# A hybrid GLA and neighbourhood-attention block on one core: the residual stream feature major from load to store

## The chip, the core and the metric

The kernel runs on one core of a Trainium2 chip. TensorE (PE) multiplies a stationary 128x128 block with a moving operand of up to 512 columns and sums in PSUM; VectorE (DVE), ScalarE (ACT) and GpSimd (POOL) work on 128 lanes; SyncE (SP) issues the transfers between DRAM and SBUF. The metric is the device time of one execution in microseconds, the median over runs.

## What is computed

Two layers over 512 latent tokens (a grid of 8 rows of 64) and 256 context tokens, width 1024, all in fp32. Layer 0 mixes tokens by gated linear attention in both directions (4 heads), layer 1 by neighbourhood attention (16 heads, latent tokens attend to a window and to the context). Each is followed by a gated feed-forward with a depthwise convolution of width 3 (2816 hidden features). Cut to what matters:

```
def modulate(x, g, shift, scale):             # rms_norm divides by the root of the mean square over features
    return rms_norm(x, g) * (1 + scale) + shift

for i in range(2):
    sh1, s1, g1, sh2, s2, g2 = split(silu(c) @ ada_w[i] + ada_b[i], 6)   # the same with c_ctx for the context
    h = modulate(x, norm1_g[i], sh1, s1)
    o = gla_mixer(h_ctx, h_lat) if i == 0 else na_mixer(h_ctx, h_lat)
    x = x + g1 * o                             # context only in layer 0
    h = modulate(x, norm2_g[i], sh2, s2)
    x = x + g2 * conv_ffn(h)                   # context only in layer 0
return rms_norm(x_lat, final_g)
# gla_mixer ends in (rms_norm(o, norm_g) * silu(r)) @ w_out, na_mixer and conv_ffn in a product with their w_out
```

## The kernel before

**Precision.** Each large product is made of three matmuls (`mm3`, L249 to L252): both operands are split into a high part and a low part (`split_to` L261: a ScalarE copy makes the high part, a VectorE subtraction the low part), and low x high, high x low and high x high are summed in PSUM. `wunit` (L234) loads a tile of weights of 128x1024, 512 KB, and splits it in the same way (L245, L246).

**Layouts.** The residual stream `X` is token major: six tiles of 128 tokens x 1024 features, two of context and four latent. What the products read, `H`, is feature major: eight tiles of 128 features x 768 tokens, high and low. So each norm turns its result: `normed` (L278) squares a token tile on ScalarE with a running sum along the row, makes the reciprocal root on GpSimd (L290, L293) and scales the row (L297); `norm_pair` (L302) turns two token tiles with TensorE (L316), applies scale and shift of the modulation, which lie along lanes then (`affine` L270), and splits.

**Gates and output products.** Token major, a gate of the residual add varies along the row. `gate_rows` (L221) therefore makes it a full 128x512 tile by TensorE (L227). Layer 0 multiplies the product with it and adds (`add_gated` L333: L338, L339); in layer 1 GpSimd multiplies the output weights with it as they are loaded (L242), and only the add remains (L335). The output products hold a token tile of activations stationary and move 512 columns of weights past it. In linear attention GpSimd also multiplies each head's result with the norm's weight `gnB` (`silu_r` L602, at L611) ahead of the product with the gate of silu (L612).

**Order of the stages.** Start: six tiles of `x` are loaded, normed, turned (L352), while `ada_first` (L129) makes the first modulation from four tiles of weights (L140, L143, L148); then the first projections. Linear attention runs head by head, `part_a` and `part_b`, levels of blocks whose decays VectorE makes (L536 to L543) for small TensorE products (L514); the last head's stretches are filled with turns and with the first half of the output product (`turn_early`). `finish_gla` reloads `x`, ends the output product and makes the second norm. `ffn` goes over 22 blocks of 128 hidden features in seven groups, six of three and one of four: two input products for each, convolution on VectorE, then the group's output product is added to `X`; in the last group the following norm (`after`) is interleaved tile by tile. Modulations for later come from `ada_lanes` (L182), in which VectorE sums weight rows (L195) in the course of other stages. Attention runs over head pairs with output products in between; its last ones are interleaved with the next norm. `final` norms a token tile and stores it.

**What sets the order.** The code is written in an order, and a list scheduler then chooses each engine's row of instructions from it; each engine works through its row strictly. Buffers are pools: three PSUM banks `mm`, five `aux`, three staging buffers for weights, five split weight tiles, four temporaries `t2`.

The split that all large products use:

```
def mm3(out, a, b, first, last):
    mm(out, a[1], b[0], start=first, stop=False)
    mm(out, a[0], b[1], start=False, stop=False)
    mm(out, a[0], b[0], start=False, stop=last)
```

## Time and profile before

| | before |
|---|---|
| median of 3 runs | 1756.88 us (1753.84 to 1758.1) |
| the profiled execution | 1755.54 us, its span 1753.8 us |
| mean granted TensorE clock | 0.993 |
| PE busy | 1695.0 us, 97% of the span |
| DVE busy | 1107.6 us, 63% |
| ACT busy | 663.1 us, 38% |
| POOL busy | 331.8 us, 19% |
| moved by DMA | 177.73 MB, mean 101 GB/s |

Busy time is a share of the whole span, and the stages have different limits, so the rows further down go by stretches. A matmul record lasts from its start to its modelled end and overlaps the next; what one costs is the spacing of starts. Where a row ends in square brackets, the engine stood idle so long before it, and the name behind the arrow is what it waited for.

### The profile page before, as it was taken

The page shows a single profiled execution, that of the slowest core. Times are in us where ns is not written, and L with a number is a line of the kernel's source. Part 1 is how long each engine was busy: PE and PEld are TensorE (multiplying, and loading weights), DVE is VectorE, ACT ScalarE, POOL GpSimd, SP SyncE. Part 2 cuts the span into 40 slices and gives each one's busy share as a digit, 9 for nine tenths or more (in the row PEclk, how much of TensorE's full clock was granted, in tenths as well). Part 3 has the DMA queues.
Part 4 walks back from the last instruction along what each step waited for, and adds up shares of the span by engine and source line. Part 5 has one row for each costly group of instructions (what it writes and reads, how often), then busy time and mean ns, then how long its engine had stood idle before and what let it go on. Part 6 is the DMA issues. An engine that isn't in the chain of part 4 may idle for free.

```text
span 1753.8 us, 26851 instructions
## 1 busy us (share of the span) xinstructions
PE 1695.0 (97%) x10783; PEld 1442.9 (82%) x10783; DVE 1107.6 (63%) x1666; ACT 663.1 (38%) x1227; POOL 331.8 (19%) x476
## 2 busy tenths in 40 slices
PE   6999999989999999999999999999999899999998
PEld 4767778777799998989899978888888788888887
DVE  4697877876656867685665484445455665566555
ACT  4675655652531221212122254443434432223322
POOL 2042423231100000000000024333442211222221
PEclk9999999999999999999999999999999999999999
DMA  8553423016122534554242212112110132233231
GB/s 292 154 169 121 148 84 113 19 49 216 49 73 92 173 112 128 181 156 142 75 132 61 73 41 88 58 41 65 54 61 25 61 115 87 87 109 108 96 96 49
DMA packets 52749, 177.73 MB, mean 101 GB/s; under 512 B 6864, under 2 KB 8784, under 8 KB 52624
## 3 DMA queue, kind: packets, MB, share of 16 engines
q1 hardware_dynamic: 52624, 176.01, 31.4%
q8 instruction: 85, 1.39, 0.3%
q14 instruction: 40, 0.33, 0.1%
HBM read 171.79 MB, written 2.10 MB: 99 GB/s over the span
## 4 chain that ended last, share of the span: by engine, by line
PE 79%; DVE 9%; ACT 4%; issue 3%; DMA 2%; POOL 2%; SPq 0%; DVEq 0%; POOLq 0%; ACTq 0%
PE mm L250 18%; PE mm L252 17%; PE mm L251 17%; PE aux L250 6%; PE aux L251 6%; PE aux L252 6%; PE mm L1013 2%; DMA sa<-in 2%; PE aux L996 2%; PE aux L971 2%; DVE t L543 1%; PE aux L623 1%; DVE t L537 1%; PE aux L316 1%; PE aux L587 1%
## 5 line engine op out<-in xcount | busy, mean ns | idle before, releaser
L250 PE MATMUL mm<-hh,wl 128*128 128x384 f32 (+3 forms) x976 | 344.7, 354 | 5.2 <-ACT hh L262 4.1
L251 PE MATMUL mm<-hl,wh 128*128 128x384 f32 (+3 forms) x976 | 340.0, 348 | 0.2
L252 PE MATMUL mm<-hh,wh 128*128 128x384 f32 (+3 forms) x976 | 339.8, 348 | 0.0
L245 ACT ACTIVATE wh<-st 128x1024 fp32r<-128x1024 f32 (+1 forms) x197 | 204.2, 1052 | 311.4 <-PE mm L252 171.2
L246 DVE TENSOR_TENSOR wl<-st,wh 128x1024 fp32r<-128x1024 f32 (+1 forms) x196 | 243.5, 1247 | 36.8 <-ACT wh L245 36.2
L250 PEld LDWEIGHTS mm<-hh,wl 128*128 128x128 f32 (+1 forms) x976 | 183.5, 188 | 27.8 <-issue 5.1
L250 PE MATMUL aux<-hh,wl 128*128 128x384 f32 (+2 forms) x576 | 200.3, 348 | 0.0
L252 PE MATMUL aux<-hh,wh 128*128 128x384 f32 (+2 forms) x576 | 200.0, 347 | 0.0
L251 PE MATMUL aux<-hl,wh 128*128 128x384 f32 (+2 forms) x576 | 199.9, 347 | 0.0
L251 PEld LDWEIGHTS mm<-hl,wh 128*128 128x128 f32 (+1 forms) x976 | 184.0, 189 | 16.8 <-DVE hl L263 1.9
L252 PEld LDWEIGHTS mm<-hh,wh 128*128 128x128 f32 (+1 forms) x976 | 183.9, 188 | 15.1
L250 PE MATMUL mm<-wh,ul 128*128 128x512 f32 (+1 forms) x444 | 176.2, 397 | 4.7 <-DVE ul L263 4.7
L251 PE MATMUL mm<-wl,uh 128*128 128x512 f32 (+1 forms) x444 | 174.9, 394 | 0.0
L252 PE MATMUL mm<-wh,uh 128*128 128x512 f32 (+1 forms) x444 | 174.3, 395 | 0.0
L242 POOL TENSOR_TENSOR st<-st,gB 128x512 f32<-128x512 f32 x60 | 94.9, 1610 | 267.3 <-DMA st<-in 139.9
L290 POOL TENSOR_SCALAR ms<-ss 128x1 f32<-128x1 f32 x26 | 9.0, 346 | 631.5 <-ACT xn L288 630.9
L250 PE MATMUL mm<-wh,hl 128*128 128x512 f32 x288 | 116.6, 405 | 0.8 <-ACT wh L245 0.8
L250 PEld LDWEIGHTS aux<-hh,wl 128*128 128x128 f32 x576 | 108.3, 188 | 9.0 <-issue 1.8
L802 ACT ACTIVATE apad<-mm 128x256 f32<-128x256 f32 (+3 forms) x90 | 36.5, 433 | 208.9 <-PE mm L252 208.9
L251 PE MATMUL mm<-wl,hh 128*128 128x512 f32 x288 | 114.8, 399 | 0.0
L251 PEld LDWEIGHTS aux<-hl,wh 128*128 128x128 f32 x576 | 108.4, 188 | 7.4 <-issue 0.4
L252 PE MATMUL mm<-wh,hh 128*128 128x512 f32 x288 | 114.3, 397 | 0.0
(211 smaller groups left out, 2826.9 us busy)
## 6 DMA issues: line engine op xcount, KB each, us to landing
st<-in SPq DMA_DIRECT2D x196, 512.0 KB, 3.7
sa<-in SPq DMA_DIRECT2D x98, 512.0 KB, 4.2
sx<-in SPq DMA_DIRECT2D x14, 512.0 KB, 6.4
xl<-in SPq DMA_DIRECT2D x8, 512.0 KB, 7.1
xc<-in SPq DMA_DIRECT2D x4, 512.0 KB, 4.4
out<-xn SPq DMA_DIRECT2D x8, 256.0 KB, 2.0
raw<-in SPq DMA_DIRECT2D x16, 96.0 KB, 2.4
t<-q SPq DMA_DIRECT2D x16, 64.0 KB, 2.1
```

The source lines that it names most:

```text
L242: nc.gpsimd.tensor_mul(st[:, s_], st[:, s_], gate[half])
L245: nc.scalar.activation(hi, st, AF.Copy)
L246: (eng or nc.vector).tensor_sub(lo, st, hi.bitcast(F32))
L250: mm(out, a[1], b[0], start=first, stop=False)
L251: mm(out, a[0], b[1], start=False, stop=False)
L252: mm(out, a[0], b[0], start=False, stop=last)
L316: nc.tensor.transpose(ps[:, o:o + 128], xs[m][k // 4][:, (k % 4) * 128:(k % 4) * 128 + 128], ident)
L537: nc.vector.tensor_sub(v(eq)[:, :, 0, :], v(bB)[:, :, 0, :], cB)
L802: nc.scalar.activation(apad[j % 2][:, pad_of(p0):pad_of(p1 - 1) + 1], ps[:, p0 - a:p1 - a], AF.Copy)
L971: mm(pss[hh][:, off:off + 256], qe[a_][p_, 128 * t:128 * t + 128], ke[b_][p_, ks], start=i == 0, stop=i == 2)
L996: nc.tensor.transpose(pT[:, i * 128:(i + 1) * 128], S2[:, o:o + 128], ident)
L1013: mm(po[64 * hh:64 * hh + 64, 128 * t:128 * t + 128], V[:, vs[i], 64 * hh:64 * hh + 64], PTs[hh][:, i * 128:(i + 1) * 128], start=i == 0, ...
```

## The change

`X` becomes feature major. `x` and `ctx` arrive turned (two context tiles that hold four feature tiles of 256 tokens each, four latent tiles that hold two feature tiles of 512 tokens each), and the output leaves as 1024 features x 512 tokens.

- A gate is then a number for each lane: `add_gated` is one VectorE instruction. `gate_rows` and the products of weights and gate are gone.
- A norm (`Norm`) sums squares over feature tiles (`add`), sums over lanes with a TensorE product with ones, makes the roots, spreads them over the lanes with a second product (`stats`), and scales, shifts and splits each feature tile (`apply`). No result of a norm is turned.
- Output products hold the weights stationary and move tokens: 8 feature tiles times a latent range of 512 and a context range of 256 tokens; in the last group of the second feed-forward and in the last one of attention two halves of 256. The first feed-forward's input products take the ranges 512 + 256 in place of 384 + 384.
- The norm weight of linear attention goes into the output weights (`scales` in `wunit`), and the product with `gnB` is gone. Five of the eight output weight tiles are loaded twice, once for each range.
- The output is stored in 16 transfers of 128 KB in place of 8 of 256 KB.

```diff
-    def wunit(src, gate=None, eng=None):
+    def wunit(src, eng=None, scales=None):
...
-        if gate:
-            for half in range(2):
-                s_ = slice(half * 512, half * 512 + 512)
-                nc.gpsimd.tensor_mul(st[:, s_], st[:, s_], gate[half])
...
+        if scales:
+            for i in range(2):
+                s_, h_, l_ = (t_.rearrange("p (k i n) -> p k i n", i=2, n=128)[:, :, i, :] for t_ in (st, hi, lo))
+                nc.scalar.activation(h_, s_, AF.Copy, scale=scales[i])
+                nc.vector.scalar_tensor_tensor(l_, s_, scales[i], h_.bitcast(F32), OP.mult, OP.subtract)
+            return hi, lo
...
-    def add_gated(pool, ps, g, xs):
-        if g is None:
-            nc.vector.tensor_add(xs, xs, ps)
-            return
-        tmp = pool.tile([128, 512], F32, name="tmp", tag="t2")
-        nc.vector.tensor_mul(tmp, ps, g)
-        nc.vector.tensor_add(xs, xs, tmp)
+    def gate(l, n, d, rng):
+        return modT[l][:, (3 * n + 2) * 8 + d, 1 if rng[1] <= N_CTX else 0:][:, 0:1]
+
+    def add_gated(ps, l, n, d, rng):
+
+        x_ = xk(d, rng)
+        nc.vector.scalar_tensor_tensor(x_, ps, gate(l, n, d, rng), x_, OP.mult, OP.add)
+
+    class Norm:
...
+        def add(self, k):
+
+            if self.acc is None:
+                self.acc = self.pool.tile([128, self.w], F32, name="nacc", tag=f"nacc{self.w}", bufs=2)
+                nc.scalar.activation(self.acc, xk(k, self.rng), AF.Square)
+                return
+            sq = self.tmp("sq")
+            nc.scalar.activation(sq, xk(k, self.rng), AF.Square)
+            nc.vector.tensor_add(self.acc, self.acc, sq)
+
+        def stats(self):
+
+            c = self.w // 128
+            ps = ps_aux()
+            for i in range(c):
+                mm(ps[:, 2 * i:2 * i + 2], self.acc[:, i * 128:(i + 1) * 128], ones, start=True, stop=True)
+            ms = sml.tile([128, 4], F32, name="ms4", tag="ms4", bufs=2)
+            nc.vector.tensor_scalar(ms[:, 0:c], ps[:, 0:2 * c:2], 1.0 / D, EPS, OP.mult, OP.add)
+            rs = sml.tile([128, 4], F32, name="rs4", tag="rs4", bufs=2)
+            nc.gpsimd.tensor_tensor(rs[:, 0:c], ms[:, 0:c], mhalf.to_broadcast([128, c]), OP.pow)
+            pb = ps_aux()
+            for i in range(c):
+                mm(pb[:, i * 128:(i + 1) * 128], rs[:, i:i + 1].to_broadcast([128, 128]), ident, start=True, stop=True)
...
+        def apply(self, k):
...
+            if self.blocks:
+                nc.vector.tensor_mul(t.rearrange("p (b r c) -> p r b c", r=8, b=8),
+                                     xk(k, self.rng).rearrange("p (r b c) -> p r b c", r=8, b=8),
+                                     self.rb.rearrange("p (r b c) -> p r b c", r=8, b=8))
+                nc.scalar.activation(t, t, AF.Identity, bias=b_, scale=a_)
+                split_to(hi, lo, t)
+                return
+            nc.vector.scalar_tensor_tensor(t, xk(k, self.rng), a_, self.rb, OP.mult, OP.mult)
+            nc.scalar.activation(hi, t, AF.Identity, bias=b_)
+            nc.vector.scalar_tensor_tensor(lo, t, b_, hi.bitcast(F32), OP.add, OP.subtract)
...
-            nc.gpsimd.tensor_mul(yh, yh, gnB)
             nc.gpsimd.tensor_mul(yh, yh, e)
...
+        lat, cx = Norm(pool, 0, 1, LAT), Norm(pool, 0, 1, CTX)
+        units = {}
+        for d in range(KD):
+            w, ps = early[d] if d < 3 else (out_unit(d), ps_mm())
+            out_part(ps, w, LAT, 6 if d < 3 else 0, KD)
+            add_gated(ps, 0, 0, d, LAT)
+            lat.add(d)
+            if d > 4:
+                units[d] = w
+        todo = lat.steps()
+        for d in (5, 6, 7, 0, 1, 2, 3, 4):
+            w = units.get(d) or out_unit(d)
             ps = ps_mm()
+            out_part(ps, w, CTX, 0, KD)
+            todo.pop(0)()
+            add_gated(ps[:, 0:N_CTX], 0, 0, d, CTX)
+            cx.add(d)
+        return todo + cx.steps()
...
-        rngs = ((0, 384), (384, 768)) if l == 0 else ((256, 768),)
+        rngs = (LAT, CTX) if l == 0 else (LAT,)
...
+                todo = []
+                for rng in (LAT, CTX) if l == 0 else ((256, 512), (512, 768)):
+                    norm = after(pool, rng)
+                    for d in range(KD):
+                        ps = out_group(d, rng)
+                        if todo:
+                            todo.pop(0)()
+                        add_gated(ps, l, 1, d, rng)
+                        norm.add(d)
+                    todo += norm.steps()
+                for f in todo:
+                    f()
...
+    class Final(Norm):
+        def apply(self, k):
+            a, b = self.rng
+            y = self.tmp("y")
+            nc.vector.scalar_tensor_tensor(y, xk(k, self.rng), sT[:, R_FG + k:R_FG + k + 1], self.rb, OP.mult, OP.mult)
+            nc.sync.dma_start(outs[0][k, :, a - N_CTX:b - N_CTX], y)
```

VectorE's row at the start, before: each token tile is scaled (`xn`) and copied back from the transposes (`xnT`), then the modulation comes (L121) and the first split.

```order
L297 TENSOR_SCALAR xn<-xl_92,rs 128x512 x2
L358 COPY xnT<-aux 128x4x128
L297 TENSOR_SCALAR xn<-xl_94,rs 128x512 x2
L246 TENSOR_TENSOR wl<-st,wh 128x512
L358 COPY xnT<-aux 128x4x128
L121 TENSOR_TENSOR mod_120<-aux,sT 128x4 x2
L126 SCALAR_TENSOR_TENSOR modA_122<-mod_120,sT 128x4
L276 TENSOR_SCALAR hf<-xnT,modA_122,mod_120 128x512 x2
L246 TENSOR_TENSOR wl<-st,wh 128x1024
L263 TENSOR_TENSOR hl<-hf,hh 128x768 x2
```

The same place after: sums of squares (`nacc`) and two means (L303) in place of scaled and copied tiles.

```order
L294 TENSOR_TENSOR nacc<-nacc,sq 128x512 x7
L303 TENSOR_SCALAR ms_159<-aux 128x4
L294 TENSOR_TENSOR nacc<-nacc,sq 128x256 x7
L303 TENSOR_SCALAR ms_196<-aux 128x2
L245 TENSOR_TENSOR wl<-st,wh 128x512
L129 TENSOR_TENSOR mod_122<-aux,sT 128x4 x2
L134 SCALAR_TENSOR_TENSOR modA_124<-mod_122,sT 128x4
L328 SCALAR_TENSOR_TENSOR hf<-xl_86,modA_124,rb 128x512
L328 SCALAR_TENSOR_TENSOR hf<-xc_84,modA_124,rb 128x256
L245 TENSOR_TENSOR wl<-st,wh 128x1024
L330 SCALAR_TENSOR_TENSOR hl<-hf,mod_122,hh 128x512
```

The modulation's sums no longer stand behind copies from transposes.

VectorE's row from the last context products of the first feed-forward (`xc`) to attention's weights (`wl`), before:

```order
L339 TENSOR_TENSOR xc_4311<-xc_4311,tmp 128x512
L263 TENSOR_TENSOR hl<-hf,hh 128x2x8x32
L338 TENSOR_TENSOR tmp<-mm,gB 128x512
L297 TENSOR_SCALAR xn<-xc_4309,rs 128x512
L339 TENSOR_TENSOR xc_4311<-xc_4311,tmp 128x512
L297 TENSOR_SCALAR xn<-xc_4309,rs 128x512
L246 TENSOR_TENSOR wl<-st,wh 128x1024 x2
L297 TENSOR_SCALAR xn<-xc_4311,rs 128x512 x2
L246 TENSOR_TENSOR wl<-st,wh 128x1024
```

After, with the latent norm's products (L322) and splits (L262) of the last feature tiles:

```order
L245 TENSOR_TENSOR wl<-st,wh 128x1024
L262 TENSOR_TENSOR hl<-hf,hh 128x512
L294 TENSOR_TENSOR nacc<-nacc,sq 128x256
L262 TENSOR_TENSOR hl<-hf,hh 128x512
L322 TENSOR_TENSOR hf<-xl_4231,aux 128x8x8x8
L294 TENSOR_TENSOR nacc<-nacc,sq 128x256
L322 TENSOR_TENSOR hf<-xl_4231,aux 128x8x8x8
L303 TENSOR_SCALAR ms_9397<-aux 128x2
L245 TENSOR_TENSOR wl<-st,wh 128x1024
L262 TENSOR_TENSOR hl<-hf,hh 128x512
L328 SCALAR_TENSOR_TENSOR hf<-xc_4226,modA_125,aux 128x256 x2
L262 TENSOR_TENSOR hl<-hf,hh 128x512
```

Latent splits and products of the norm now stand behind and between the first weights of attention.

VectorE's last rows, before:

```order
L335 TENSOR_TENSOR xl_4317<-xl_4317,mm 128x512 x2
L299 SCALAR_TENSOR_TENSOR xn<-xl_4317,rs,fgB 128x512 x2
L335 TENSOR_TENSOR xl_4319<-xl_4319,mm 128x512
L335 TENSOR_TENSOR xl_4319<-xl_4319,mm 128x256 x2
L299 SCALAR_TENSOR_TENSOR xn<-xl_4319,rs,fgB 128x512 x2
```

And after:

```order
L273 SCALAR_TENSOR_TENSOR xl_4231<-mm,mod_123,xl_4231 128x256
L1109 SCALAR_TENSOR_TENSOR y<-xl_4231,sT,aux 128x256
L294 TENSOR_TENSOR nacc<-nacc,sq 128x256
L303 TENSOR_SCALAR ms_15933<-aux 128x2
L1109 SCALAR_TENSOR_TENSOR y<-xl_4228,sT,aux 128x256 x2
L1109 SCALAR_TENSOR_TENSOR y<-xl_4229,sT,aux 128x256 x2
L1109 SCALAR_TENSOR_TENSOR y<-xl_4230,sT,aux 128x256 x2
L1109 SCALAR_TENSOR_TENSOR y<-xl_4231,sT,aux 128x256 x2
```

Eight outputs of 256 columns stand behind the last mean, where two of 512 stood behind the last root.

## Rows read from the trace of the kernel before

**Rows 1.** Stretches: window, length, busy time of PE, PEld, DVE, ACT, POOL, clock, DMA
```profile
25.00:66.70 41.70, 39.12 (x273) 29.68 (x274) 17.99 (x38) 18.34 (x29) 3.10 (x5) 0.96 0.60 190
66.70:365.00 298.30, 275.77 (x2784) 218.18 (x2784) 247.95 (x371) 184.63 (x379) 93.44 (x94) 0.99 0.34 109
...
1005.00:1060.00 55.00, 54.47 (x268) 43.99 (x267) 41.53 (x70) 27.65 (x59) 14.30 (x32) 1.00 0.22 70
...
1365.00:1400.00 35.00, 30.81 (x208) 26.91 (x207) 20.23 (x34) 17.63 (x39) 9.47 (x20) 1.00 0.24 76
```

**Rows 2.** Timeline of PE: start, length, instruction, shape; pairs that span equal matmuls
```profile
702.06 0.33 PE L250 MATMUL mm<-hh,wl 128*128 128x384 f32 x1
...
704.66 0.33 PE L250 MATMUL mm<-hh,wl 128*128 128x384 f32 x1
...
1371.97 0.98 PE L316 MATMUL aux<-ident,xn 128*128 128x128 f32 x7 [1.07 <-DVE xn L297]
1372.71 0.48 PE L250 MATMUL mm<-wh,ol 128*128 128x512 f32 x1
...
1392.54 0.28 PE L250 MATMUL aux<-hh,wl 128*128 128x256 f32 x1
...
1395.41 0.28 PE L250 MATMUL aux<-hh,wl 128*128 128x256 f32 x1
...
1419.95 0.39 PE L250 MATMUL mm<-wh,ul 128*128 128x512 f32 x1
...
1421.77 0.39 PE L252 MATMUL mm<-wh,uh 128*128 128x512 f32 x1
```

**Rows 3.** Start: timeline of PE, and DMA rate of the first 20 us
```profile
23.32 1.07 PE L140 MATMUL mm<-sx,cs 128*32 128x256 f32 x16
...
28.60 0.56 PE L250 MATMUL mm<-hh,wl 128*64 128x384 f32 x2 [2.38 <-ACT hh L262]
...
GB/s 0 0 0 90 90 185 372 295 393 221 213 262 385 328 377 401 393 418 434 418 410 418 410 418 434 410 410 410 426 426 410 401 401 410 401 410 418 410 426 401
```

**Rows 4.** Linear attention: PE's waits (sum, times, longest), a group, timelines of DVE, POOL
```profile
PE aux L514 <- DVE t L543: 10.4, 10, 3.1
...
L611 POOL TENSOR_TENSOR xl<-xl,gnB 128x256 f32<-128x256 f32 x16 | 27.2, 1701 | 50.1 <-DVE er L609 41.1 <-DVE mod L118 5.8 <-ACT t L541 3.1
...
339.59 1.40 POOL L611 TENSOR_TENSOR xc<-xc,gnB 128x256 f32<-128x256 f32 x1 [1.76 <-DVE er L609]
...
340.31 1.09 DVE L536 TENSOR_TENSOR t<-b 128x384 f32<-128x384 f32 x1
...
342.25 0.55 DVE L537 TENSOR_TENSOR t<-b 128x384 f32<-128x384 f32 x1
```

**Rows 5.** First feed-forward: timeline of PE at and behind a stall
```profile
677.21 0.50 PE L250 MATMUL mm<-wh,ul 128*128 128x512 f32 x1 [2.10 <-DVE ul L263]
...
678.34 0.63 PE L251 MATMUL mm<-wl,uh 128*128 128x512 f32 x1
...
681.33 0.49 PE L250 MATMUL mm<-wh,ul 128*128 128x512 f32 x1
```

**Rows 6.** VectorE's groups by line and shape: sum, mean ns, idle before them
```profile
L246 DVE TENSOR_TENSOR wl<-st,wh 128x1024 fp32r<-128x1024 f32 x195 | 242.8, 1250 | 36.8 <-ACT wh L245 36.2
...
L338 DVE TENSOR_TENSOR tmp<-mm,gB 128x512 f32<-128x512 f32 x96 | 66.1, 690 | 38.9 <-PE mm L252 38.7
...
L843 DVE TENSOR_TENSOR u<-tt,aux 128x256 f32<-128x256 f32 x30 | 12.1, 419 | 17.0 <-ACT tt L838 17.0
...
L629 DVE SCALAR_TENSOR_TENSOR xl<-aux,rs,xl 128x256 f32<-128x256 f32 x16 | 7.5, 480 | 13.1 <-POOL rs L258 13.0
```

**Rows 7.** The end: timeline of PE, POOL and DVE
```profile
1746.81 0.28 PE L252 MATMUL mm<-wh,uh 128*128 128x256 f32 x1
...
1748.66 0.55 POOL L293 TENSOR_TENSOR rs<-ms,mhalf 128x1 f32<-128x1 f32 x1
...
1749.24 1.41 DVE L299 SCALAR_TENSOR_TENSOR xn<-xl,rs,fgB 128x512 f32<-128x512 f32 x2 [1.70 <-POOL rs L293]
```

## The prediction before the run

> **What bounds the kernel now.** I read the table of stretches first [rows 1]: TensorE is busy 275.77 of 298.30 us in the linear-attention stretch, 54.47 of 55 us at the border from the first feed-forward to neighbourhood attention, 30.81 of 35 us at the border behind that attention, and it fills the rest but for the start and the last microseconds. VectorE is busy 247.95 of 298.30 us in linear attention and about three quarters of the time at the first of these borders. So TensorE's own work sets the time, and an edit elsewhere counts only where TensorE waits: at the start, inside linear attention, at the borders where a norm must be finished, and behind the last matmul. The prediction is a sum over these places, made against the profiled run's 1755.54 us, which stands 1.3 us below the median of 1756.88.
>
> **TensorE's work: -9.0.** Records overlap, so I take the spacing of starts [rows 2]: eight 512-wide matmuls in 1.82 us are 0.2275 us each, fifteen 384-wide in 2.60 are 0.173, twenty-four 256-wide in 2.87 are 0.120, and seven 128-wide fp32 records in 0.74 are 0.106. The orders of both kernels, counted, give 1944 more split matmuls of 256 columns, 1920 fewer of 384 and 468 more of 512: +232.5 - 332.7 + 106.5 = +6.3. (384 + 384 becomes 512 + 256 in the first feed-forward, and the output groups that had 512 columns of weights moving now have 512 or 256 tokens moving.) Gone are 128 transposes (L316) outside the start, -13.6, and 48 gate broadcasts (L227) of two records each, -10.2. New are, for each of 20 blocks of 128 tokens outside the start, a sum over lanes (L301) and a broadcast (L308), two records each: +8.5. Spacings read from two rows may be off by 0.005 us, and 468 and 1944 of them make 2 us: I keep -9, from -11 to -7.
>
> The Trainium skill (TensorE: Matmul & The Clock Gate, Back-to-back issue gap) gives N/2.4 + 2.5 ns for an isolated warm matmul, an estimate of 109, 162 and 216 ns for these widths; the rows show about 11 more for each. By it the column term would be +1 and the sum 5 us lower. Its sustained 131 ns for 512 columns is not what these rows show.
>
> **The start: -5, from -6 to -2.** The modulation matmuls that the first products need (L140) end at 24.4, because TensorE takes them between the transposes; then copy, small matmuls, scale, affine and split lead to the first product at 28.60, 4.2 us later [rows 3]. The transfers run at about 400 GB/s from the fifth microsecond [rows 3] (its columns are 0.5 us each); summed, the 5.5 MB of constants, x and the first four modulation tiles have landed at about 17. The changed start has no transposes, and its norm sums hide: eight squares of 512 and eight of 256 on ScalarE follow the x tiles and end near 13.5, statistics near 16. So the modulation matmuls could end near 18.5, the same chain follows, and the first product comes near 23. TensorE then has nearly nothing to wait for until 66.7 (39.12 of 41.70, 2.4 of the rest before the first product), so the gain is kept. -2 if the sums queue ahead of the modulation copies.
>
> **Linear attention: -4, from -8 to 0.** TensorE waits 10.4 us for the decay products (L543) of VectorE there [rows 4]. GpSimd's multiplication by the norm weight (L611, 16 of 1.70 us on the latent half, 8 like them on the context) goes into the output weights. While it runs, a subtraction of two SBUF operands takes 1.09 instead of 0.55 us: the one at 340.31 begins inside the product at 339.59, the one at 342.25 does not overlap it [rows 4]. One such stretch of 0.54 for each of 24 is 13 us of VectorE's time. VectorE is the later engine only in the levels where TensorE waits, so about a third passes on. 0 if the scheduler's order, not VectorE's pace, makes these waits; -8 with the clock's part below.
>
> **A stall costs more than its length.** After the 2.10 us wait in the first feed-forward the 512-wide matmuls are spaced 0.427 us from 678.34 to 681.33, the lower of the clock's two levels (1.2 against 2.4 GHz) [rows 5]: seven by 0.2 more than in [rows 2] are 1.4 us on top. I count this for stalls over 2 us.
>
> **End of linear attention: 0, from -1 to +2.** A context group is 24 matmuls, 2.88 us. VectorE's work for one is a scaled weight tile (the 1.25 of L246, here in two halves with a scalar), two ops of 512 columns for the latent half, one gated 256 (0.48) and one add (0.42): 3.3 [rows 6]. Five of the eight groups load weights anew; the deficit of 5 by 0.4 is covered by the three that do not.
>
> **First feed-forward: +1, from -3 to +5.** The 2.10 us stall there is a wait for a split (L263) [rows 5], in whose row on VectorE the sums of the next modulation (L195, over weights that come from DRAM) stand. These jobs stay. The gate drops from two VectorE ops of 0.69 to one for each block [rows 6], but VectorE doesn't bound these groups, so that is worth nothing; the work ahead of the third split shrinks by about 0.7, so such a stall may grow by that, come twice more with its slow clock, or vanish with it (3.5).
>
> **First feed-forward to neighbourhood attention: +4.5, from +1 to +7.** Before, TensorE is full there [rows 1]. Now the context range comes last: a group is four products in three parts of 256 columns, 1.44 us, and beside each VectorE has a gated 256, an add of 256, a latent product and a latent split of 512: 0.40 + 0.34 + 0.61 + 0.61 = 1.96, from 0.48, 0.42 and twice 0.69 [rows 6] less about 0.08 of overlap each. Eight by 0.52 leave VectorE 4.2 us late, and the weights of attention (1.25 each) and the last latent splits stand behind that in its row. Three accumulators in PSUM let TensorE run ahead, but it then waits at the first projection. Lower end: the scheduler's filling; upper: plus 1.4 of slow clock.
>
> **Attention to the second feed-forward: -1, from -2 to +2.** 35 - 30.81 = 4.2 us of waits are there now [rows 1], behind scale, transpose, affine and split. The last output group in two token halves gives 0.72 us of TensorE against 1.5 of VectorE for each of 16; one half's norm hides beside the other, the second doesn't, about 3.
>
> **The end: +3.5, from +3 to +4.** Now the last matmul starts at 1746.81, the reciprocal root at 1748.66, and the two scaled outputs run from 1749.24 to 1750.65 [rows 7]; 3.1 remain to the span's end. After: gated 0.48, square, add 0.42, lane sum, mean, root 0.55, broadcast, then eight outputs of 256 columns at 0.40 (the four y buffers make the second four wait for transfers), and the same 3.1: about 10.2 from the last matmul's end against 6.7.
>
> **Sum.** -9 - 5 - 4 + 0 + 1 + 4.5 - 1 + 3.5 = -10: a profiled run of 1745.5, a median of 1746. The unknown ends, taken as independent, give 1739 to 1754.
>
> **Rivals.** *VectorE becomes the bound at every norm border (slower).* Price: the whole excess of the last range at each: 5 by 0.7 at the end of linear attention, 4.2 plus 3 of queued weights ahead of attention, 16 by 0.78 behind it, and 1.4 of slow clock at three places, 27 in place of the 3.5 counted: 1769 at worst, 1764 if a quarter hides. It decides if VectorE's share per group exceeds TensorE's by more than the three accumulators cover. For it: 1.96 against 1.44. Against it: the scheduler may put next-stage products between. *The gains at the waits don't land (same).* Linear attention gives 0, the start -2, the border costs 7: -9 - 2 + 0 + 0 + 1 + 7 - 1 + 3.5 = -0.5, 1756. For it: TensorE's waits there follow a hand-made interleave. *GpSimd's product holds VectorE for its whole length.* Then 24 by 1.6 = 39 us of VectorE come free, and all 10.4 us of waits behind L543 go, with the slow clock after the longest: -13 in place of -4, 1737. For it: ops in its shadow double. Against it: 0.54 lost, not 1.4 [rows 4].
>
> The Trainium skill (SBUF — State Buffer, Who interferes with whom) has this third rival as a rule: VectorE reads a second SBUF operand through a port shared with GpSimd, and whichever op comes second is blocked fully. Here the stretch is shorter than the GpSimd op's 1.40 us, so the rows bear out sharing, not a hold over the whole length.
>
> **Chances.** Forecast 0.55, VectorE-bound borders 0.15, no gain at the waits 0.17, full release 0.13. A measurement of this kernel can tell about 0.3%, 5.3 us, from no change. Faster: 0.8 of the forecast, all of the full release, a fifth of "no gain", 0.60. Same: the rest of the forecast, 0.7 of "no gain", a quarter of the slow rival, 0.27. Slower: 0.13. The range 1735 to 1761 takes in the forecast, "no gain", most of the full release and the near side of the slow rival, and leaves out about 0.15.
>
> **What would show it.** In the profile after: first product at 22 to 24; waits behind the decay products near 6 in linear attention; no stall over 1 us at the end of linear attention; one stall of 3 to 6 us where attention's first projections begin, with VectorE's splits or weights as releaser; 3 us in sum behind attention; 10 us from the last matmul to the end. The forecast is wrong if the first product stays near 28, if the borders lose over 12 us together, or if TensorE's sum does not fall by about 9.

## The result, and the profile after

The changed kernel takes 1740.78 us in the median of 6 runs (1738.64 to 1748.47); the kernel before took 1757.24 beside it (1753.3 to 1758.27). The ratio of the mean times, here as for every run below, is 0.9918, with a 95% interval of 0.9896 to 0.994. Between the medians 16.5 us were gained, between the means 14.4, where 11 were forecast. The profiled run took 1739.42 us with a span of 1737.6, 16.2 below the span before.

The table of stretches, cut at the same places in both kernels: start, first product, first decay product, last V·t product of linear attention, first and last modulation sum of the first feed-forward, first scores and end of neighbourhood attention, last matmul, end. The columns are those of [rows 1]: window, length, busy time of PE, PEld, DVE, ACT, POOL, granted clock, DMA share, GB/s. Before:

```profile
0.00:28.60 28.60, 13.85 (x91) 10.29 (x91) 14.14 (x34) 16.66 (x39) 7.27 (x26) 1.00 0.89 321
28.60:90.40 61.80, 60.40 (x403) 45.44 (x403) 36.13 (x63) 33.08 (x59) 3.10 (x5) 0.97 0.52 168
90.40:394.50 304.10, 281.43 (x2783) 224.51 (x2783) 245.38 (x371) 180.02 (x374) 100.64 (x107) 0.98 0.32 101
394.50:560.60 166.10, 163.04 (x862) 141.55 (x861) 101.43 (x148) 56.35 (x104) 9.86 (x29) 1.00 0.30 102
560.60:910.30 349.70, 345.00 (x1856) 318.98 (x1855) 238.66 (x301) 79.22 (x118) 0.00 (x0) 0.99 0.45 142
910.30:1067.60 157.30, 156.77 (x831) 140.49 (x831) 93.18 (x138) 53.39 (x98) 16.98 (x36) 1.00 0.20 63
...
1358.60:1747.10 388.50, 383.79 (x1802) 319.13 (x1800) 230.17 (x275) 125.68 (x185) 80.88 (x70) 1.00 0.28 90
1747.10:1753.80 6.70, 0.00 (x0) 0.00 (x0) 1.83 (x3) 0.71 (x4) 1.16 (x4) 0.71 0.21 79
```

And after:

```profile
0.00:29.45 29.45, 11.95 (x67) 8.31 (x67) 13.10 (x32) 13.30 (x26) 2.71 (x11) 0.97 0.82 306
29.45:92.40 62.95, 61.21 (x400) 45.31 (x400) 44.42 (x78) 32.74 (x60) 3.33 (x5) 0.96 0.51 166
92.40:383.00 290.60, 277.41 (x2784) 221.10 (x2784) 234.63 (x378) 181.12 (x379) 72.38 (x83) 1.00 0.34 106
383.00:543.00 160.00, 156.00 (x907) 137.62 (x906) 101.38 (x152) 55.43 (x89) 5.85 (x14) 0.99 0.39 122
543.00:887.80 344.80, 343.10 (x2000) 297.99 (x1999) 212.69 (x255) 78.69 (x104) 0.00 (x0) 1.00 0.46 144
887.80:1045.30 157.50, 154.69 (x875) 135.16 (x875) 86.12 (x130) 53.69 (x84) 7.92 (x16) 0.99 0.20 62
...
1335.80:1726.60 390.80, 385.62 (x1908) 324.87 (x1908) 224.68 (x330) 125.31 (x183) 3.21 (x7) 1.00 0.28 86
1726.60:1737.60 11.00, 1.32 (x8) 1.04 (x8) 5.03 (x13) 0.42 (x1) 0.69 (x1) 0.70 0.34 119
```

Row by row the lengths differ by +0.85, +1.15, -13.5, -6.1, -4.9, +0.2, +2.3 and +4.3; neighbourhood attention itself, left out here, by -0.5. Linear attention gave most of the gain, at the same count of matmuls: TensorE's idle time (length less busy) fell from 22.7 to 13.2, and its busy time by 4.0 with the granted clock, 0.98 to 1.00. VectorE's busy time fell by 10.8. The start gave nothing. The waits of TensorE (sum, times, longest), the third of which answers to [rows 4]:

```profile
PE aux L301 <- DVE nacc L294: 10.3, 3, 8.5
PE aux L308 <- POOL rs L305: 8.6, 10, 1.5
PE aux L497 <- DVE t L526: 5.8, 7, 1.1
```

The third row was 10.4 before, under L514 and L543. The first two are new (8.5 of the first is at the start, where TensorE waits for the first sums): the sums over lanes and the broadcasts of a norm wait for VectorE's squares and for GpSimd's roots.

### The profile page after: what moved, and what is told of

Same layout as the page of the kernel before. It is cut to its first block, busy times and chain, and to the rows that moved or that the text cites. A ratio compares the mean times of both kernels' runs of the same rounds, so it can differ in the third digit from the quotient of the medians.

```text
span 1737.6 us, 27175 instructions
## 1 busy us (share of the span) xinstructions
PE 1681.7 (97%) x11107; PEld 1413.8 (81%) x11107; DVE 1070.4 (62%) x1699; ACT 658.7 (38%) x1173; POOL 190.9 (11%) x324
## 4 chain that ended last, share of the span: by engine, by line
PE 80%; DVE 10%; ACT 4%; DMA 2%; issue 2%; POOL 1%; SPq 0%; POOLq 0%; DVEq 0%; ACTq 0%
PE mm L249 18%; PE mm L251 17%; PE mm L250 17%; PE aux L249 6%; PE aux L250 6%; PE aux L251 6%; PE mm L1006 2%; DMA sa<-in 2%; PE aux L989 2%; PE aux L964 2%; DVE t L526 1%; PE aux L605 1%; PE aux L570 1%; DVE acc L203 1%; DVE t L525 1%
## 5 line engine op out<-in xcount | busy, mean ns | idle before, releaser
L249 PE MATMUL mm<-hh,wl 128*128 128x512 f32 (+3 forms) x1104 | 388.6, 354 | 3.9 <-ACT hh L329 2.5
L251 PE MATMUL mm<-hh,wh 128*128 128x512 f32 (+3 forms) x1104 | 383.3, 348 | 0.0
L250 PE MATMUL mm<-hl,wh 128*128 128x512 f32 (+3 forms) x1104 | 383.0, 347 | 0.0
L249 PE MATMUL aux<-hh,wl 128*128 128x512 f32 (+2 forms) x576 | 201.1, 349 | 0.0
L250 PE MATMUL aux<-hl,wh 128*128 128x512 f32 (+2 forms) x576 | 201.0, 349 | 0.0
L251 PE MATMUL aux<-hh,wh 128*128 128x512 f32 (+2 forms) x576 | 200.8, 349 | 0.0
L249 PE MATMUL mm<-uh,wl 128*128 128x512 f32 (+1 forms) x560 | 194.1, 350 | 1.7 <-ACT uh L261 1.4
L250 PE MATMUL mm<-ul,wh 128*128 128x512 f32 (+1 forms) x560 | 194.2, 348 | 0.0
L251 PE MATMUL mm<-uh,wh 128*128 128x512 f32 (+1 forms) x560 | 193.3, 346 | 0.0
L273 DVE SCALAR_TENSOR_TENSOR xl<-mm,mod,xl 128x512 f32<-128x512 f32 (+1 forms) x168 | 116.3, 698 | 108.9 <-PE mm L251 108.6
L250 PEld LDWEIGHTS aux<-hl,wh 128*128 128x128 f32 x576 | 109.2, 190 | 14.4 <-issue 1.1
```

What stands on the lines that cost most here:

```text
L273: nc.vector.scalar_tensor_tensor(x_, ps, gate(l, n, d, rng), x_, OP.mult, OP.add)
```

## Experiments

**Linear attention: what did the missing product give?** Two kernels put a GpSimd product of the same size back into the changed kernel, against a tile of ones. In `g_chain` it stands where the old one stood, in the chain of the output; in `g_side` its result goes to a scratch tile that nobody reads. `b_nogn` is the kernel before without L611.

`g_chain`:

```diff
+            nc.gpsimd.tensor_mul(yh, yh, oneB)
             nc.gpsimd.tensor_mul(yh, yh, e)
```

> The changed kernel with one GpSimd product of 128x256 put back for each head and token tile (24 in all), by a tile of ones, in the place where the product with the norm's weight stood. Linear attention is 13.4 us shorter after the change than before. Theory A, VectorE's two-operand instructions are slowed while the product runs and VectorE sets the pace at nearly every wait there: 8 to 13 us slower than the changed kernel, back near 1750. Theory B, the step of the prediction, where only a third of it passes on: 3 to 5 us slower. Theory C, the scheduler's other order made the gain, not the product: within 2 us of the changed kernel.

`g_side`:

```diff
             nc.gpsimd.tensor_mul(yh, yh, e)
+            sc = pool.tile([128, DV], F32, name="sc", tag="sc", bufs=1)
+            nc.gpsimd.tensor_mul(sc, yh, oneB)
```

> The changed kernel with the same 24 GpSimd products of two SBUF operands, written to a scratch tile behind the product with the gate, so that nobody waits for them. Theory A, contention with VectorE is what counts: the same 8 to 13 us as with the product in the chain, VectorE's subtractions of 384 columns at a mean over 0.62 us. Rival D, the product costs because the head's result comes later: within 2 us of the changed kernel, though the other run lost 8 or more.

`b_nogn`, against the kernel before:

```diff
-            nc.gpsimd.tensor_mul(yh, yh, gnB)
             nc.gpsimd.tensor_mul(yh, yh, e)
```

> The kernel before without GpSimd's product with the norm's weight, which leaves that weight out of the result. Theory A: 8 to 13 us faster than the kernel before, with waits behind the decay products near 6 us in place of 10.4. Theory B: 3 to 5 us faster. Theory C: within 2 us of the kernel before.

The table of stretches for linear attention, one row of each, in this order:

```profile
93.40:397.00 303.60, 283.09 (x2784) 226.35 (x2784) 246.60 (x378) 181.51 (x379) 98.81 (x107) 0.98 0.33 102
```
```profile
92.10:392.70 300.60, 279.85 (x2784) 223.77 (x2784) 246.39 (x378) 181.59 (x379) 96.53 (x107) 0.99 0.33 103
```
```profile
90.60:385.00 294.40, 278.80 (x2783) 222.01 (x2783) 233.95 (x371) 180.31 (x374) 69.26 (x83) 0.99 0.33 105
```

Put back in the chain, the product costs 13.0 us of this stretch; put back beside the chain, 10.0; taken out of the kernel before, it gives 9.7. In the kernels below that leave this place alone the stretch takes 290.6 to 294.3, so a difference of 3 to 4 us here shows nothing. The whole times follow: `g_chain` 1750.28 against 1754.72 (0.9965, 0.9949 to 0.9982), `g_side` 1747.60 (0.9956, 0.9939 to 0.9972), `b_nogn` 1745.51 (0.9938, 0.9915 to 0.9962); `g_side` is 6.8 above the changed kernel's median, a little under the 8 that theory A asked for. Most of the gain of linear attention is the missing product, 9.7 to 13.0 us of 13.5, and it works by what it does to VectorE, since the scratch product, for which nobody waits, costs nearly as much. Nor does it make the chain's own products late: of GpSimd's 47.5 us of idle time before those of the latent half, 47.4 are waits for ScalarE. The longer chain explains 3 us at most, which is within the spread. One row of TensorE's waits in `g_side`, of the decay products behind VectorE:

```profile
PE aux L499 <- DVE t L528: 6.1, 7, 1.1
```

That is hardly more than the 5.8 of the changed kernel, though the stretch is 10 us longer: VectorE's loss came out at other waits and in the granted clock (0.99 for 1.00).

**The start: why no gain?** TensorE's timeline of the changed kernel (start, length, instruction, shape, idle before):

```profile
13.08 1.84 PE L301 MATMUL aux<-ones,nacc 128*128 128x2 f32 x8 [8.52 <-DVE nacc L294]
16.37 2.07 PE L308 MATMUL aux<-ident,rs 128*128 128x128 f32 x8 [1.45 <-POOL rs L305]
18.68 1.02 PE L301 MATMUL aux<-ones,nacc 128*128 128x2 f32 x4 [0.23 <-DVE nacc L294]
19.62 1.06 PE L148 MATMUL mm<-sx,cs 128*32 128x256 f32 x2
21.12 1.22 PE L308 MATMUL aux<-ident,rs 128*128 128x128 f32 x4 [0.43 <-POOL rs L305]
22.27 2.96 PE L148 MATMUL mm<-sx,cs 128*32 128x256 f32 x30
...
29.45 0.90 PE L249 MATMUL mm<-hh,wl 128*64 128x384 f32 x2 [2.46 <-ACT hh L329]
```

The modulation's matmuls (L148) end at 25.23, and the first product follows 4.2 us later, as before. Both norms' statistics stand ahead of 30 of the 32 modulation matmuls in TensorE's row. Their four groups last 6.15 us in sum, the first broadcast 2.07 for eight records where [rows 2] show 0.106 for one, and each broadcast waits for roots that GpSimd makes in 1.1 us. ScalarE's last squares come late too, for want of buffers, which come free as VectorE adds; VectorE itself stood 2.02 us at the latent range's mean, for TensorE's sums over lanes. A row of ScalarE, and one of GpSimd:

```profile
15.48 1.48 ACT L293 ACTIVATE sq<-xc 128x256 f32<-128x256 f32 x3 [2.10 <-DVE nacc L294]
```
```profile
15.20 1.12 POOL L305 TENSOR_TENSOR rs<-ms,mhalf 128x4 f32<-128x4 f32 x1 [14.11 <-DVE ms L303]
```

`s_both` writes the modulation's matmuls ahead of the statistics and gives the squares four buffers of their own. `n_ln` shortens the statistics in place: one product of a 128x128 tile of ones with the sums spreads the mean to all lanes at once, and ScalarE makes the root as exp(-0.5 ln). `n_ln_y` adds buffers to it: four and seven for the squares, twelve for the output.

`s_both`:

```diff
+        first = ada_first(0, pool)
         norms = [Norm(pool, 0, 0, rng, spread=True) for rng in (LAT, CTX)]
...
                 norm.add(k)
+        for norm in norms:
             norm.stats()
...
-        ada_first(0, pool)()
+        first()
```

> The changed kernel with the first modulation's matmuls written ahead of the first norm's statistics, both statistics behind both sums, and four staging buffers of their own for the squares of each range. The changed kernel's first product is at 29.45 us, not near 23 as predicted. Theory E, the statistics of the context range stand ahead of the modulation matmuls in TensorE's row, and its sums wait for buffers and for a mean on VectorE: first product at 24 to 26, 3 to 5 us faster than the changed kernel, the gain kept to the end. Rival F, transfers or ScalarE's squares set the start: first product over 28.5, within 1 us.

`n_ln`, in `stats`, with `ones` 128x128:

```diff
-            c = self.w // 128
-            ps = ps_aux()
...
+            ps = ps_aux()[:, 0:self.w]
+            mm(ps, ones, self.acc, start=True, stop=True)
+            self.rb = self.acc
+            nc.scalar.activation(self.rb, ps, AF.Ln, bias=epsc, scale=1.0 / D)
+            nc.scalar.activation(self.rb, self.rb, AF.Exp, scale=-0.5)
```

> The changed kernel with another way through the statistics: one product of a 128x128 tile of ones with the summed squares gives the sum over lanes on every lane at once, and ScalarE makes the reciprocal root by Ln and Exp, in place of lane sum, mean on VectorE, power on GpSimd and broadcast product. s_both left the first product at 30.4 us; the modulation matmuls still stood behind statistics in TensorE's row. Theory E, the statistics in TensorE's row set the start: first product at 23.5 to 25.5, 4 to 6 us of the sum; the end shorter by 1.3, the waits at roots (8.6 us in 10 places) mostly gone, TensorE's statistics cheaper by about 4; in all 8 to 13 us faster than the changed kernel, 1728 to 1733. Rival F, transfers, squares and sums set the start: first product over 28, in all 3 to 7 us faster.

`n_ln_y`, besides:

```diff
+                sq = self.pool.tile([128, self.w], F32, name="sq", tag=f"sq{self.w}", bufs=4 if self.w == 512 else 7)
...
-            y = self.tmp("y")
+            y = self.pool.tile([128, self.w], F32, name="y", tag="y", bufs=12)
```

> n_ln with twelve buffers of their own for the outputs and with four and seven of their own for the first norm's squares. The last eight outputs wait 0.65 us for earlier transfers, and ScalarE waits about 2 us for square buffers at the start. Theory: the end 0.6 us shorter, the first product up to 1.5 us earlier than in n_ln if the context range's sum is last there, 0 if the modulation's transfers are. Rival: transfers follow each other at their own rate at the end, no change.

`s_both` took 1738.90 (0.9899, 0.9875 to 0.9924), but its first product came at 30.4: the expectation missed. The scheduler still wove the statistics into the modulation in TensorE's row: 24 of its 32 matmuls stand behind the second sum over lanes, 16 behind the last broadcast. It doesn't settle the start; its 3 us lie elsewhere and are within what stretches without an edit vary by. `n_ln` moved the first product to 24.94:

```profile
12.76 2.04 PE L301 MATMUL aux<-nacc,ones 128*128 128x512 f32 x2 [7.80 <-DVE nacc L296]
...
17.33 3.30 PE L150 MATMUL mm<-sx,cs 128*32 128x256 f32 x32
24.94 0.90 PE L251 MATMUL mm<-hh,wl 128*64 128x384 f32 x2 [2.53 <-ACT hh L321]
```

The modulation ends at 20.63, 4.6 earlier than in the changed kernel, and the first product follows 4.3 behind it. So the statistics in TensorE's row were what held the start. `n_ln` took 1734.12 (0.988, 0.9865 to 0.9894), `n_ln_y` 1732.22 (0.9876, 0.9859 to 0.9892); the added buffers did not bring the first product further forward (26.5). The price of Ln and Exp shows at the norms of layer 1. ScalarE's timeline at the end of `n_ln_y`:

```profile
1718.84 1.28 ACT L306 ACT_TABLE_LOAD   x1
```

A second load of 1.28 us stands at 1721.22, before the Exp. The last matmul stood 12.4 us from the end, and 13.3 in `n_ln`, where the changed kernel has 11.0 and 1.3 less were expected; the way from the feed-forward to attention took 160.5 instead of 157.5.

**The first feed-forward: which edit gave 4.9?** `u_384` gives the input products their ranges 384 + 384 again; `f_two` makes the gate two VectorE instructions again; `f_both` does both.

`u_384`:

```diff
+        rin = RNG if l == 0 else (LAT,)
...
-                for rng in rngs:
+                for rng in rin:
                     in_group(j, 0, w0, rng)
...
-                u = finish(j, [in_group(j, 1, w1, rng) for rng in rngs])
+                u = finish(j, [in_group(j, 1, w1, rng) for rng in rin])
```

> The changed kernel with the input products of the first feed-forward (all but the first two hidden blocks) in ranges of 384 and 384 tokens as before; the output products keep 512 and 256. The first feed-forward from its first modulation sum to its last is 5 us shorter after the change than before, and the two stalls behind splits, 4.7 us and their slow clock, are gone. Theory H, the gate as one instruction frees VectorE and so removes them: within 2 us of the changed kernel. Rival I, the ranges do it, by the order in which halves of the convolution come free: 4 to 8 us slower, with stalls over 2 us behind the splits.

`f_two`:

```diff
         x_ = xk(d, rng)
+        if l == 0 and n == 1:
+            tmp = sml.tile([128, 512], F32, name="tmp", tag="tmp", bufs=1)[:, 0:rng[1] - rng[0]]
+            nc.vector.tensor_scalar(tmp, ps, gate(l, n, d, rng), None, OP.mult)
+            nc.vector.tensor_add(x_, x_, tmp)
+            return
```

> The changed kernel with the gate of the first feed-forward as two VectorE instructions again (a product with the lane's scalar into a temporary, then the add). Theory H, one instruction in place of two frees VectorE and so removes the two stalls behind splits: from the first to the last modulation sum (542 to 890 us) 4 to 8 us longer than in the changed kernel, stalls of 2 us behind splits back, 1745 to 1750. Rival, VectorE has room there and the stalls went with the new order of the groups: within 1.5 us in that stretch, though the border to attention may lose 2.

`f_both` has both edits.

> The changed kernel with both the two-instruction gate of f_two and the 384 + 384 input ranges of u_384, to see whether the two stalls behind splits in the first feed-forward need both. Theory J, they do: from the first to the last modulation sum 348 to 352 us, stalls of 2 us or more behind splits. Rival K, the output products' new form (weights stationary, groups by feature tile) removed them: 345 to 347 us, waits behind splits at 2 us in sum, as in u_384.

The table of stretches between the first and the last modulation sum, of `u_384`, `f_two` and `f_both`:

```profile
545.50:891.70 346.20, 342.85 (x2000) 323.76 (x1999) 214.04 (x269) 79.32 (x118) 0.00 (x0) 1.00 0.45 143
```
```profile
544.00:888.90 344.90, 343.84 (x2000) 297.48 (x1999) 248.83 (x319) 78.59 (x104) 0.00 (x0) 1.00 0.46 144
```
```profile
548.10:899.40 351.30, 345.90 (x2000) 324.97 (x2000) 250.15 (x333) 79.40 (x118) 0.00 (x0) 1.00 0.46 141
```

Alone, the ranges cost 1.4 us and the gate 0.1; together 6.5, back to the kernel before (349.7). Other kernels that leave this stretch alone show 342.4 to 344.8, so the single edits show little here, and the theory by which the gate's one instruction alone brings the gain in this stretch falls. Either edit suffices for the length. TensorE's waits behind splits there, in the kernel before and in `f_both`:

```profile
PE mm L250 <- DVE ul L263: 4.7, 2, 2.6
...
PE mm L250 <- DVE ul L262: 2.0, 2, 1.2
```

So `f_both` has the length of theory J and the waits of rival K: it is as long as the kernel before, but the two stalls of over 2 us did not come back. Short waits are there instead, 5.4 us in sum with these, none over 1.2, where the changed kernel has 1.7. So neither of the two edits is what removed the two stalls; the output products' new form, rival K, is left, with the scheduler's new order, and no run undoes them. Why the loss comes only when both edits are undone is open too: `f_both` has VectorE 250 us busy of 351, and so has `f_two`, 249 of 345, without the loss. `u_384` took 1742.85 (0.9928, 0.9913 to 0.9943), `f_both` 1752.00 (0.9975, 0.9963 to 0.9987).

`f_two` still lost some 7 us of the gain (1748.11, 0.996, 0.9945 to 0.9975), most of it at the border behind this stretch, which took 162.3 instead of 157.5. TensorE's timeline there:

```profile
1022.03 0.76 PE L249 MATMUL mm<-hh,wl 128*128 128x512 f32 x1 [3.42 <-DVE tmp L275]
1023.01 0.63 PE L251 MATMUL mm<-hh,wh 128*128 128x512 f32 x1
1023.44 0.63 PE L249 MATMUL mm<-hh,wl 128*128 128x512 f32 x1
```

A stall of 3.42 us behind the gate's product, and matmuls 0.43 apart behind it: the lower clock, as in [rows 5]. It has the place and the size of the stall that the prediction expected of the changed kernel itself, though its releaser is the gate's product and no split or weight; there, the gate's one instruction keeps it away.

**The border behind attention: who holds it?** `b_noadd` leaves out 14 of the 16 squares and all 14 adds of the norm there, so that its root is that of one feature tile.

```diff
+            if self.l == 1 and self.n == 1 and k < KD - 1:
+                return
```

> The changed kernel with the squares and sums of the norm between attention and the second feed-forward left out for all but the last feature tile of each half (14 squares, 14 adds), so that its result is not the reference's. Theory V, VectorE bounds that border: 14 adds at 0.34 to 0.42 are 5 us of its work, 2.5 to 5 us faster. Rival W, the chain of lane sum, mean, power, broadcast bounds it: within 1 us.

```profile
1334.90:1721.40 386.50, 384.43 (x1908) 323.56 (x1908) 220.29 (x315) 119.88 (x169) 3.20 (x7) 1.00 0.28 87
```

The row is that of the stretch from the end of attention to the last matmul. It took 386.5 where the changed kernel has 390.8 and eight others with the same norm there 389.3 to 390.8; the whole time was 1734.82 (0.9893, 0.9869 to 0.9918). VectorE's busy time is 4.4 less and the stretch 3 to 4 shorter. TensorE's waits for the gated adds in the first 45 us of the stretch, in the changed kernel and in `b_noadd`:

```profile
PE mm L249 <- DVE xl L273: 2.6, 3, 1.7
...
PE mm L249 <- DVE xl L273: 0.3, 1, 0.3
```

The waits for roots fell from 1.7 to 0.9 as well, and the granted clock of these 45 us rose from 0.96 to 1.00. So the making of the sums, on VectorE (36 of the 45 us busy) behind ScalarE's squares (23), holds most of this border; the run leaves out both kinds of op and doesn't part them. The chain of rival W has a share: `n_ln` and `n_ln_y`, which shorten it and keep every add, took 387.3 and 387.9. But they do so by 3 to 4 us less of TensorE's busy time; their idle time in the stretch, 5.5, is no less than the changed kernel's 5.1.

**A faster kernel.** `n_mix` keeps Ln and Exp for the norms of layer 0 alone, with the buffers of `n_ln_y`. `n_dve` also moves the last GpSimd product of linear attention to VectorE.

`n_mix`, with the buffers:

```diff
+            if self.l == 0:
+                ps = ps_aux()[:, 0:self.w]
+                mm(ps, ones, self.acc, start=True, stop=True)
...
+                return
             c = self.w // 128
```

> n_ln_y with Ln and Exp for the norms of layer 0 alone; the norms of layer 1 keep mean, power and broadcast product. In n_ln and n_ln_y ScalarE loads a function table for nearly every Ln and every Exp of layer 1 (1.28 us each), and TensorE waits 4.8 and 4.3 us at the borders of attention. Theory: these loads cost about 2.5 us at the first border and 1.5 at the end, while the second border and TensorE's cheaper statistics gave about 3 back; 1728 to 1732, first product at 25 to 26.5. Rival: the borders are bound by VectorE's other work and the loads hide, within 1 us of n_ln_y.

`n_dve`, besides:

```diff
-            nc.gpsimd.tensor_mul(yh, yh, e)
+            nc.vector.tensor_mul(yh, yh, e)
```

> n_mix with the last GpSimd product of linear attention (result by gate of silu, 128x256, 24 times, 1.1 to 1.9 us each) on VectorE. Theory A, from g_chain and g_side: the product's shadow costs VectorE about 0.5 us each, 12 us, against 24 by 0.34 of its own, and the head's result comes 1 us earlier: linear attention 2 to 5 us shorter than in n_mix, subtractions of 384 columns at a mean of 0.57 in place of 0.64, 1724 to 1727. Rival: VectorE paces linear attention and 8 us more work on it cost more than the shadow: 2 to 5 us slower than n_mix.

`n_mix` took 1729.14 against 1756.35 (0.9852, 0.9832 to 0.9872), `n_dve` 1728.34 against 1757.02 (0.9835, 0.9817 to 0.9853). Both beat the changed kernel, by about 12 us; between them the intervals overlap, and `n_dve` missed its 1724 to 1727. In `n_dve` nothing stretches VectorE's subtractions any more:

```profile
L535 DVE TENSOR_TENSOR t<-b 128x384 f32<-128x384 f32 x28 | 15.4, 551 | 0.0
```

Before, the costliest line of these four had a mean of 773 ns, and after 668. But the 24 products now take VectorE's own time, its busy sum stays (234.3 against 234.9 in `n_mix`), and the stretch takes 291.5 against 294.3, within the spread.

## Why the prediction was right in sum and wrong in its terms

The forecast, 1746, was 5 us above the measured median, inside the range; several terms were wrong and cancelled in part, so that the total came out near is in part luck. By one of its own signs, a first product that stays near 28, the forecast is wrong: it came at 29.45. Where a length is given below, it holds TensorE's own work too, which the sum had as a term of its own; idle time is then the fairer measure.

- **TensorE's work, -9.** Its busy sum fell from 1695.0 to 1681.7, by 13.3; 4.0 of that is the clock in linear attention, with the same matmuls. Another 1.9 is the start, which the term left out. The 7.4 left lie at the near end of the term's -11 to -7, and 1.9 of them are the first feed-forward, where the slow clock behind two stalls went; how much more of it is clock can't be told.
- **The start, -5, measured +0.85, and +1.15 more up to the first decay product.** The step that failed is that the norm's sums "hide" and the modulation could end near 18.5. It ended at 25.23, since the sums were costed on ScalarE and VectorE and not as entries in TensorE's row ahead of the modulation, with a root of 1.1 us on GpSimd between. The row of the changed order on TensorE would have shown it. The 4.2 us from the modulation to the first product held, in both kernels and in `n_ln`. The bound of -2, for sums that queue ahead of the modulation's copies, was not wide enough. (In [rows 3] the rate is near 400 GB/s only from about 7 us on; the 5.5 MB by 17 hold.)
- **Linear attention, -4, measured -13.5.** The price of VectorE's loss was right: 13 us were counted, 10.8 came free. The step that failed is "about a third passes on". By `b_nogn`, `g_side` and `g_chain`, VectorE's 11.4, 11.8 and 12.0 us (busy time against the kernel that each was made from) became 9.7, 10.0 and 13.0 of the stretch. The waits behind the decay products fell to 5.8, as forecast (near 6); but they are one row among several, and TensorE's idle time fell by 9.5 in all, its clock's loss by 4.0. What VectorE loses passes on nearly whole in this stretch, not in the levels alone in which TensorE's longest wait is seen.
- **The reading of [rows 4] as sharing was wrong**, though the 0.54 lost for each product stands. The next section has the rows.
- **End of linear attention, 0.** From the last V·t product to the first modulation sum 6.1 us went, 7.0 of TensorE's busy time, and idle time rose by 0.9. No stall over 1 us was forecast there; the longest is 1.3, behind VectorE's last results of a head, as before (1.4). 1.8 are waits for roots, and `n_ln_y`, which has none, took 155.3 for the 160.0, 3.2 of it in TensorE's busy time.
- **First feed-forward, +1, measured -4.9.** The gate's saving was called worth nothing, "VectorE doesn't bound these groups". With the new ranges that is true (0.1, `f_two`); with the old ones the gate's one instruction is worth 5.1 (`f_both` against `u_384`). That a stall might vanish (3.5) was in the range; both did, and the sum put it on the other side.
- **To attention, +4.5.** Idle time rose by 2.3 (0.5 to 2.8), and the length by 0.2. The step that failed is VectorE's lateness: no stall of 3 to 6 us came, and of the 2.8 none is put down to VectorE. What came instead was a wait at the two broadcasts for GpSimd's roots, a link that the term did not have:

```profile
PE aux L308 <- POOL rs L305: 2.0, 2, 1.2
```

The other 0.7 is behind a copy of ScalarE. With the gate as two instructions the stall did come (3.42).
- **Behind attention, -1, measured +2.3.** Of the 2.3, 1.8 are TensorE's busy time, with 106 matmuls more, and 0.5 idle time (4.7 to 5.2), where the term had 1 less. The step "one half's norm hides beside the other" gave too much: 5.0 us of waits are there and not 3, 2.6 of them for VectorE's gated adds, 1.7 for roots, and `b_noadd` takes most of the first away. The slow clock behind the longest of them, granted 0.68 in the 5 us from 1355.8, is part of the busy time.
- **The end, +3.5, measured +4.3.** Rows that answer to [rows 7]:

```profile
1728.09 0.61 PE L301 MATMUL aux<-ones,nacc 128*128 128x2 f32 x4 [1.53 <-DVE nacc L294]
1729.04 0.69 POOL L305 TENSOR_TENSOR rs<-ms,mhalf 128x2 f32<-128x2 f32 x1 [12.26 <-DVE ms L303]
1729.79 0.71 PE L308 MATMUL aux<-ident,rs 128*128 128x128 f32 x4 [1.09 <-POOL rs L305]
1730.54 1.66 DVE L1109 SCALAR_TENSOR_TENSOR y<-xl,sT,aux 128x256 f32<-128x256 f32 x4 [1.64 <-PE aux L308]
1732.84 1.95 DVE L1109 SCALAR_TENSOR_TENSOR y<-xl,sT,aux 128x256 f32<-128x256 f32 x4 [0.65 <-DMA out<-y]
```

The chain is the one that was written down, most links a little longer. The wait of 0.65 for the output's buffers is worth little: with twelve of them `n_mix` has 10.8 us from the last matmul to the end.

Of the rivals, "full release" came nearest in time (1737) and by place, for another reason than its price of 39 us: 11 us of VectorE came free, nearly all of it passed on, and 5.8 of the 10.4 us of waits stayed. The slow rival's mechanism, VectorE at the borders, is real at one of them, behind attention, for the 2.6 us of waits and the slow clock behind them, and not for 27 in sum.

## What to carry to other kernels

Where an engine feeds the bounding one all through a stretch, count what it gains or loses in full, as with VectorE, busy for 235 to 245 of some 300 us here, and not by the share of the waits that carry its name. An op that is moved to other engines still has entries in the row of the engine that bounds: read the new order there before you cost it at nothing. A small tail of dependent ops (sum, power, broadcast) at each norm costs more than its ops' sizes tell (8.6 us of waits for roots at ten places here), and is worth shortening by one link.

## What the runs showed of the hardware

**A GpSimd product and a VectorE op with two SBUF operands exclude each other.** GpSimd's and VectorE's timelines of `g_side`, and of the kernel before:

```profile
335.63 1.21 POOL L596 TENSOR_TENSOR xc<-xc,er 128x256 f32<-128x256 f32 x1 [9.10 <-ACT er L595]
336.91 0.93 POOL L598 TENSOR_TENSOR sc<-xc,oneB 128x256 f32<-128x256 f32 x1
...
336.16 1.09 DVE L522 TENSOR_TENSOR t<-b 128x384 f32<-128x384 f32 x1
337.18 1.09 DVE L523 TENSOR_TENSOR t<-b 128x384 f32<-128x384 f32 x1
```
```profile
352.47 4.14 POOL L611 TENSOR_TENSOR xl<-xl,gnB 128x256 f32<-128x256 f32 x1 [3.77 <-DVE er L609]
...
356.19 0.84 DVE L537 TENSOR_TENSOR t<-b 128x384 f32<-128x384 f32 x1
```

The products end at 336.84 and 337.84, the two subtractions at 337.25 and 338.27, 0.41 and 0.43 later; in the kernel before at 356.61 and 357.03, and [rows 4] at 340.99 and 341.40. The next, at 338.19 with no product beside it, takes 0.54. In the kernel before, 26 subtractions held up by a product all end 0.41 or 0.42 behind its end, and four of twice the width 0.82; 38 of the 48 products there end 0.59 to 0.61 behind a VectorE op that was there first, as the second one above does behind the subtraction that ended at 337.25. A product with no VectorE op beside it takes 0.72 to 0.73 (291.36 and 292.16 in the kernel before); the 0.93, the 1.40 and the 4.14 hold its own wait for VectorE, so GpSimd's recorded lengths don't tell what it costs VectorE. That is about 0.54 for each product, however long its record. The one of 4.14 waited through six VectorE ops in a row, up to 356.01, and the one in [rows 4] through one; why is not shown. The Trainium skill (SBUF — State Buffer, Who interferes with whom) has the port between the two as an exclusive lock: whoever comes second is blocked fully. The rows bear it out, against the reading in the prediction.

**Small ops with large prices.** GpSimd's power took 1.12 us on 128x4 and 1.09 on 128x2 at the start, 0.69 to 1.61 on 128x2 later, where the root of one column takes 0.55 in [rows 7]; so its width alone doesn't set its record. In layer 1 of `n_ln_y` ScalarE loads a table of 1.28 us for Ln and again for Exp. The Trainium skill (ScalarE: Activation LUTs, Table sets: the hidden batching unit) has both functions in one set, with one load. Both ways are seen in `n_ln_y`: up to 471 us, in layer 0, 36 Ln stand among its Exp with no load but the first, at 0.7 us, as the Trainium skill has it; at the norms of layer 1 loads stand before both lines, six each. Why layer 1 was built with a load for each is not shown; `n_mix`, which keeps Ln and Exp to layer 0, has none of these twelve loads.
